# Hybrid decoder layer on one core: the output projection as seven products of quarters, and an order planned with GpSimd's and VectorE's shared port

## Chip, cores and metric

One core of a Trainium2 chip. The metric is the device time of one execution in microseconds (us). PE is TensorE's matmuls, PEld its weight loads, DVE is VectorE, ACT is ScalarE, POOL is GpSimd, SP is SyncE, which issues most of the DMAs.

## What is computed

One layer of a decoder for 1024 rows of 1024, in float32. Two attention mixers run beside each other; their outputs are projected, gated, merged, and projected again:

```python
h = rmsnorm(x, g_pre[i])
proj = h @ w_in[i]                              # queries, keys, values and gates of mixers A and B
y_a = (att_a * silu(gate_a)) @ w_branch_a[i]    # A: indexer, top-k keys, sparse attention
y_b = (att_b * silu(gate_b)) @ w_branch_b[i]    # B: forgetting attention
m_a, m_b = split(sigmoid(h @ w_merge[i]))
out = (m_a * y_a + m_b * y_b) @ w_out[i]        # the output projection, 1024x1024 @ 1024x1024
x = x + rmsnorm(out, g_post[i])
e = p[i] @ w_ple[i]
gate = sigmoid(x @ w_ple_gate[i])
x = x + rmsnorm(gate * e, g_ple[i])
```

## The kernel before

The kernel records every operation of the layer in a list (`Program`), plans an order for them, and only then issues them, all from one line (L521). So the profile's rows carry that line, and the tiles are parts of three arenas: `arena_r` (operands of matmuls), `arena_f` (float32) and `arena_p` (the eight PSUM banks).

Every matmul is done as three: a float32 operand is split into a rounded part `hi` (a cast, on ACT or DVE) and a rest `lo` (a subtraction, on POOL or DVE), and `mm3` adds `hi*hi + hi*lo + lo*hi` into one bank. Where two engines are given for an operation (`split_w`, `either`), the planner takes the one that finishes first by its costs (`_cost`). It keeps a free time per engine, and takes the earliest operation whose inputs, arena space and bank are there; the priority `BASE` of its part breaks ties. `QUOTA` bounds the space of each group of tiles: weights of the last stages (`wo`) have 56 KB, seven tiles, and their staging buffers (`st`) 8 KB, two of 4 KB.

The program goes: the projections and the indexer's scores (to about 260 us), four pairs of heads of mixer B with the top-k search beside them, mixer A with the merge gates `pm` filling PE between its steps, then the end, in which this order holds:

- branch projections, `y1_j_t` and `y0_j_t` for 8 column blocks j of the merged rows and 2 halves t of the rows: 4 x 3 matmuls each. DVE multiplies by the gates, adds, and the sum is split into `mt`. `at1...` are mixer B's results, loaded back by POOL's DMAs.
- the embedding `pe`, 16 blocks of 2 x 3 matmuls, stored in HBM (`ge_d`).
- the output projection `out{q}_{b}`: 2 halves q of the columns by 8 row blocks b, each 8 x 3 matmuls of 128x512. Its weights come in eight tiles, `wo0*` and `wo1*` (`load_q`), each half a float32 load of 512 KB, a cast and a subtraction. Per block DVE scales the bank into `x1` and ACT sums the squares. After q = 1 the block's residual follows: root, reciprocal, two scalings with the residual's addition in them, eight transposes `xt`, cast and difference into `xT`.
- the last gate `pg{q}_{b}`, again 2 x 8 blocks of 8 x 3 matmuls, with weights `wg0*` and `wg1*`, then the last norm and the stores.

The first gate blocks need `xT` of the first four row blocks alone. At the time of `pg0_0` the order before still has `xt7` ahead of it or in it.

## Time and profile before

| | |
|---|---|
| median of 3 runs | 1109.43 us (1109.23 to 1111.66) |
| profiled execution | 1111.12 us, its span 1109.4 us |
| PE / PEld busy | 97% / 80% of the span |
| DVE / ACT / POOL busy | 72% / 54% / 12% |
| DMA | 128.00 MB, 115 GB/s in the mean |
| mean granted clock of PE | 0.986 of full speed |

The span runs from the first to the last instruction. A busy share is a mean over stages with different limits. In the stage's tables each engine has its busy time and its number of instructions, PEclk is the granted clock (1.00 is 2.4 GHz, 0.50 is 1.2 GHz). In timelines a row merges operations of one kind that follow each other; in brackets stands the idle time of the engine ahead of them, and the engine whose work ended it. Operations of one engine overlap by some 0.08 us, so the distance between two starts tells what one costs in a queue.

### The profile page before, as it was taken

Reading aid. Unit: us, or ns where it says so; the run is one execution under the profiler, and the core shown is the slowest. Engines: PE = TensorE matmul, PEld = TensorE weight load, DVE = VectorE, ACT = ScalarE, POOL = GpSimd, SP = SyncE. Lnnn points to the kernel's source line nnn. Section 1 sums busy time; section 2 is a strip of 40 time slices with the busy share of each in tenths; the row PEclk is TensorE's granted clock in tenths of the full one; section 3 lists DMA queues with packets and bytes.
Section 4 is the critical chain, followed back from the end, with each engine's and each line's share of the span. In section 5 each row is a group of like instructions: output and inputs, shape, how many; then the busy total and the mean of one; then the engine's idle time right before and its main releaser. Section 6 shows DMA issues by size and latency. Waiting matters only on the chain. (4 is left out here: it accounts for less than half of the span.)

```text
span 1109.4 us, 16308 instructions
## 1 busy us (share of the span) xinstructions
PE 1073.3 (97%) x5290; PEld 882.7 (80%) x5290; DVE 802.1 (72%) x2086; ACT 603.8 (54%) x1396; POOL 133.2 (12%) x244
## 2 busy tenths in 40 slices
PE   8899999999999999999999999999999999999995
PEld 6777887887878878788878888888888888887884
DVE  6999667757969878799999957655388732366277
ACT  6565578888889889775278855432112131233212
POOL 1413000010111211211411200000100000000011
PEclk8999999999999999999999999999999999998998
DMA  7212033370361622635243422333786273026032
GB/s 264 70 37 67 11 138 119 134 180 10 102 156 39 159 70 82 150 97 178 95 124 97 122 64 79 106 113 106 227 247 200 77 242 109 29 72 202 31 111 99
DMA packets 117594, 128.00 MB, mean 115 GB/s; under 512 B 11642, under 2 KB 78330, under 8 KB 117508
## 3 DMA queue, kind: packets, MB, share of 16 engines
q1 hardware_dynamic: 105940, 108.60, 30.7%
q0 software_dynamic: 11568, 18.35, 7.1%
q8 instruction: 42, 0.69, 0.3%
q14 instruction: 44, 0.36, 0.1%
HBM read 89.60 MB, written 33.13 MB: 111 GB/s over the span
## 5 line engine op out<-in xcount | busy, mean ns | idle before, releaser
L521 PE MATMUL arena_p<-arena_r 128*128 128x512 f32 (+5 forms) x4384 | 1016.0, 385 | 17.1 <-DVE arena_r L521 6.5
L521 PEld LDWEIGHTS arena_p<-arena_r 128*128 128x128 f32 x4384 | 783.8, 190 | 175.6 <-DVE arena_r L521 11.3
L521 ACT ACTIVATE arena_f<-arena_p 128x512 f32<-128x512 f32 (+5 forms) x188 | 97.9, 533 | 205.9 <-PE arena_p L521 123.7
L521 DVE TENSOR_TENSOR arena_r<-arena_p,arena_r 128x512 fp32r<-128x512 f32 (+3 forms) x232 | 141.7, 622 | 48.4 <-ACT arena_r L521 44.7
L521 ACT CAST arena_r<-arena_p 128x512 fp32r<-128x512 f32 (+4 forms) x217 | 107.3, 516 | 117.7 <-PE arena_p L521 114.1
L521 ACT ACTIVATE arena_f<-arena_f,cnd 128x1024 bf16<-128x1024 f32 (+4 forms) x160 | 149.7, 936 | 31.9 <-DVE cnd L521 28.1
L521 ACT ACTIVATE arena_f<-arena_f,stats 128x512 f32<-128x512 f32 (+3 forms) x192 | 116.9, 611 | 21.2 <-DVE stats L521 15.8
L521 DVE TENSOR_TENSOR arena_r<-arena_f,arena_r 128x512 fp32r<-128x512 f32 (+4 forms) x200 | 120.0, 612 | 4.3 <-ACT arena_r L521 1.0
L521 PE MATMUL arena_p<-ident,arena_f 128*128 128x128 f32 x720 | 110.7, 276 | 1.8 <-DVE arena_r L521 0.6
L521 POOL TENSOR_TENSOR arena_r<-arena_f,arena_r 128x512 fp32r<-128x512 f32 (+2 forms) x51 | 65.4, 1289 | 366.2 <-ACT arena_r L521 111.4
L521 PEld LDWEIGHTS arena_p<-ident,arena_f 128*128 128x128 f32 x720 | 87.4, 142 | 24.0 <-DVE arena_f L521 2.3
L521 ACT CAST arena_r<-arena_f 128x512 fp32r<-128x512 f32 (+3 forms) x104 | 55.1, 561 | 69.2 <-DVE arena_f L521 45.8
L521 DVE CAST arena_r<-arena_f 128x512 fp32r<-128x512 f32 (+3 forms) x147 | 55.1, 384 | 41.5 <-DMA arena_f<-in_w_out_dram 15.2
L521 DVE CUSTOM_DVE_ANT_0 arena_f<-arena_p,arena_f 128x512 f32<-128x512 f32 (+2 forms) x112 | 64.1, 577 | 2.6 <-PE arena_p L521 1.5
L521 DVE SCALAR_TENSOR_TENSOR arena_f<-arena_f,wi 128x384 f32<-128x384 f32 (+3 forms) x70 | 48.3, 696 | 13.4 <-ACT arena_f L521 12.6
L521 POOL TENSOR_SCALAR_AFFINE_SELECT arena_f<-arena_f 128x128 f32<-128x128 f32 x70 | 22.5, 323 | 260.5 <-DVE stats L521 112.8
L521 DVE SCALAR_TENSOR_TENSOR arena_f<-arena_f,arena_p 128x512 f32<-128x512 f32 x48 | 32.8, 683 | 28.9 <-PE arena_p L521 22.1
L521 DVE CAST arena_r<-arena_p 128x512 fp32r<-128x512 f32 (+4 forms) x67 | 40.8, 612 | 17.7 <-PE arena_p L521 17.4
L521 ACT COPY arena_f<-arena_p 64x256 f32<-64x256 f32 (+5 forms) x85 | 37.8, 445 | 21.7 <-PE arena_p L521 17.9
L521 DVE SCALAR_TENSOR_TENSOR arena_f<-arena_f 128x512 f32<-128x512 f32 (+7 forms) x47 | 29.0, 623 | 26.5 <-ACT arena_f L521 25.6
L521 DVE TENSOR_TENSOR arena_f<-arena_f 128x512 f32<-128x512 f32 (+3 forms) x101 | 45.0, 446 | 1.3 <-DMA arena_f<-rd_d 0.5
L521 DVE CUSTOM_DVE_ANT_0 arena_f<-arena_p,arena_f,stats 128x384 f32<-128x384 f32 (+2 forms) x64 | 39.3, 615 | 6.9 <-PE arena_p L521 3.6
(103 smaller groups left out, 486.1 us busy)
## 6 DMA issues: line engine op xcount, KB each, us to landing
arena_f<-in_w_in_dram SPq DMA_DIRECT2D x56, 256.0 KB
arena_f<-in_w_merge_dram SPq DMA_DIRECT2D x32, 256.0 KB
th_d<-arena_f SPq DMA_DIRECT2D x32, 256.0 KB
arena_f<-th_d SPq DMA_DIRECT2D x32, 256.0 KB
arena_f<-in_x_dram SPq DMA_DIRECT2D x18, 256.0 KB
vb_d<-arena_r SPq DMA_DIRECT2D x8, 512.0 KB
qsa_d<-arena_r SPq DMA_DIRECT2D x16, 256.0 KB
arena_f<-negc_d SPq DMA_DIRECT2D x8, 512.0 KB
```

What stands on the lines that cost most here:

```text
L521: getattr(eng[x], m)(*[real(q) for q in a], **{n: real(q) for n, q in k.items()})
```

## The change

The output projection becomes seven products of quarters instead of eight. The merged rows are cut in four quarters of 512 x 512 (A11 is rows 0 to 511 by columns 0 to 511), the weights too (B11 ...). With the sums S1 = A21+A22, S2 = S1-A11, S3 = A11-A21, S4 = A12-S2 and T1 = B12-B11, T2 = B22-T1, T3 = B22-B12, T4 = B21-T2 the products P1 = A11 B11, P2 = A12 B21, P3 = S4 B22, P4 = A22 T4, P5 = S1 T1, P6 = S2 T2, P7 = S3 T3 are formed (four blocks of 128 rows each, 4 x 3 matmuls a block). The output's quarters are P1+P2, P1+P6+P5+P3, P1+P6+P7+P4 and P1+P6+P5+P7, added up on DVE, ACT and in PSUM: P2 is accumulated onto P1's banks after these were copied out, P4 onto P7's.

The sums of the rows are formed in the branch stage as its blocks come out. The sums of the weights are formed on POOL alone, 16 subtractions of 128x512 in four rounds through one tile of 8 KB, and stored in HBM (`tw_d`); each round's two loads of 512 KB also wait for a weight load of one of the last eight merge gates. The scaling by `g_post` moves from the PSUM read into the residual, whose addition becomes an operation of its own.

The planner gets a rule: an operation of DVE with SBUF inputs alone (with a few exceptions) and a two-input operation of POOL don't overlap in the plan. Some quotas grow (`wn`, `we`, `xr`), `vbt` gets its reserve earlier.

```diff
+def _port(eng, method, a, k):
+    ins = [q for q in list(a[1:]) + list(k.values()) if isinstance(q, Ref) and q is not k.get("out")]
+    big = [q for q in ins if q.shape[1:] != (1,)]
+    if eng == "G":
+        return method.startswith("tensor_") and len(big) > 1
+    if eng != "V" or any(q.t.space == "P" for q in ins) or method in ("memset", "tensor_tensor_reduce", "tensor_tensor_scan"):
+        return False
+    return len(big) > 1 or "accum_out" not in k
...
+        def starts(op, e):
+            s = max(free[e], op.r[e])
+            return max(s, port["G" if e == "V" else "V"]) if op.port[e] else s
...
-                    s = max(t0, op.r[e])
+                    s = starts(op, e)
...
+    def weight_sums(w, dst, after):
+        for k in range(4):
+            b4 = pg.tile([P, 4, 512], F32, "tw", f"tw{k}")
+            for g in range(2):
+                SY.dma_start(b4[:, 2 * g:2 * g + 2].rearrange("p a b -> p (a b)"), w[(4 * g + k) * P:(4 * g + k + 1) * P, :])
+                pg.ops[-1].deps.add(after[k])
+            G.tensor_sub(b4[:, 0], b4[:, 1], b4[:, 0])
+            G.tensor_sub(b4[:, 1], b4[:, 3], b4[:, 1])
+            G.tensor_sub(b4[:, 3], b4[:, 3], b4[:, 0])
+            G.tensor_sub(b4[:, 2], b4[:, 2], b4[:, 3])
+            SY.dma_start(dst[:, k], b4)
+    weight_sums(w_out[0], tw_d[0], gate_at[8:12])
...
-            V.tensor_add(ths[0], ths[0], ths[1])
-            split_w(ths[0], mt[t][0][j // 4][:, j % 4], mt[t][1][j // 4][:, j % 4])
+            m = mq[t][j]
+            V.tensor_add(m, ths[0], ths[1])
+            if t == 0:
+                left["A11" if j < 4 else "A12"].append(halves(m, "mA", f"mA{j}"))
+            elif j < 4:
+                either("tensor_sub", s3[j], mq[0][j], m)
+            else:
+                q = j - 4
+                either("tensor_add", mq[1][q], mq[1][q], m)
+                either("tensor_sub", mq[0][q], m, s3[q])
+                either("tensor_sub", mq[0][j], mq[0][j], mq[0][q])
...
+    for n, src in (("S2", mq[0][:4]), ("S1", mq[1][:4]), ("S4", mq[0][4:]), ("S3", s3), ("A22", mq[1][4:])):
+        for k in range(4):
+            left[n].append(halves(src[k], "mS", f"{n}{k}"))
...
+    ws, open_ = wquad("B11"), []
+    for i in range(4):
+        open_.append(product(left["A11"], i, ws, "P1", [x1[4 + i]]))
+        A.copy(part[i], open_[i])
+    ws = wquad("B21")
+    for i in range(4):
+        A.copy(x1[i][:, q0], product(left["A12"], i, ws, "P2", [x1[i]], open_[i]))
+        square(i, 0)
+    ws = wquad("T2")
+    for i in range(4):
+        add_to(part[i], product(left["S2"], i, ws, "P6"), part[i])
+    ws, ws2 = wquad("T1"), wquad("B22")
+    for i in range(4):
+        add_to(late[i], product(left["S1"], i, ws, "P5"), part[i])
+        add_to(x1[i][:, q1], product(left["S4"], i, ws2, "P3"), late[i])
+        square(i, 1)
+        first_residual(i)
+    ws, open_ = wquad("T3"), []
+    for i in range(4):
+        open_.append(product(left["S3"], i, ws, "P7"))
+        add_to(late[i], open_[i], late[i])
+        square(4 + i, 1)
+    ws = wquad("T4")
+    for i in range(4):
+        add_to(part[i], product(left["A22"], i, ws, "P4", (), open_[i]), part[i])
+        square(4 + i, 0)
+        first_residual(4 + i)
...
-        for k in range(KC):
-            mm3(ps, mt[t][0][k // 4][:, k % 4, bs], mt[t][1][k // 4][:, k % 4, bs], *wq[q][k],
-                k == 0, k == KC - 1, [x1[b]] if k == 0 else ())
-        V.scalar_tensor_tensor(x1[b][:, cq], ps, 0.25, gpb[:, cq], op0=ALU.mult, op1=ALU.mult)
-        A.activation(jo, ps, AF.Square, scale=0.25, accum_out=s1[:, b, q:q + 1])
```

`product` runs the 4 x 3 matmuls of one block, `add_to` adds a bank to a tile on DVE, `square` sums squares on ACT from `x1`, `first_residual` is the block's residual as above, `quad` loads and splits the two weight tiles of a quarter.

Where instructions stand now, at three places. First PE, from the last blocks of the output projection to the end. Rows of 128x128 are the transposes `xt` of the residual blocks, all others matmuls of the projection or, at the end, of the gate. Before:

```order
L521 MATMUL arena_p<-arena_r 128x512 x15
L521 MATMUL arena_p<-ident,arena_f 128x128 x4
L521 MATMUL arena_p<-arena_r 128x512 x9
L521 MATMUL arena_p<-ident,arena_f 128x128 x4
L521 MATMUL arena_p<-arena_r 128x512 x6
L521 MATMUL arena_p<-ident,arena_f 128x128 x4
L521 MATMUL arena_p<-arena_r 128x512 x21
L521 MATMUL arena_p<-ident,arena_f 128x128 x4
L521 MATMUL arena_p<-arena_r 128x512 x357
```

and now:

```order
L541 MATMUL arena_p<-arena_r 128x512 x12
L541 MATMUL arena_p<-ident,arena_f 128x128 x4
L541 MATMUL arena_p<-arena_r 128x512 x15
L541 MATMUL arena_p<-ident,arena_f 128x128 x4
L541 MATMUL arena_p<-arena_r 128x512 x15
L541 MATMUL arena_p<-ident,arena_f 128x128 x4
L541 MATMUL arena_p<-arena_r 128x512 x6
L541 MATMUL arena_p<-ident,arena_f 128x128 x4
L541 MATMUL arena_p<-arena_r 128x512 x324
```

384 matmuls belong to the gate. So the last transposes moved from 27 matmuls into the gate to 60 matmuls into it, two and a half blocks.

Second DVE at the hand-over. Rows of 128x1024 from `arena_f` are the splits of the gate's weights, rows of 128x512 from `arena_p` are reads of a product's bank, those of 128x4x128 differences for `xT`, `s_164` holds the sums of squares and what follows from them. Before:

```order
L521 SCALAR_TENSOR_TENSOR arena_f<-arena_p,arena_f 128x512
L521 TENSOR_TENSOR s_164<-s_164 128x1
L521 CAST arena_r<-arena_f 128x1024
L521 TENSOR_TENSOR arena_r<-arena_p,arena_r 128x4x128
L521 RECIPROCAL s_164<-s_164 128x1
L521 TENSOR_TENSOR arena_r<-arena_f,arena_r 128x1024
L521 SCALAR_TENSOR_TENSOR arena_f<-arena_f,s_164 128x512
L521 TENSOR_TENSOR arena_r<-arena_f,arena_r 128x1024
```

and now:

```order
L541 SCALAR_TENSOR_TENSOR arena_f<-arena_p,arena_f 128x512
L541 TENSOR_TENSOR arena_r<-arena_f,arena_r 128x1024 x2
L541 TENSOR_TENSOR arena_r<-arena_p,arena_r 128x4x128
L541 SCALAR_TENSOR_TENSOR arena_f<-arena_p,arena_f 128x512
L541 TENSOR_TENSOR arena_r<-arena_f,arena_r 128x1024
L541 SCALAR_TENSOR_TENSOR arena_f<-arena_p,arena_f 128x512
L541 TENSOR_TENSOR arena_r<-arena_f,arena_r 128x1024
```

The first bank read shown before is that of the last output block; the first one now is that of the third block of P7, with P4's four still to come. The weights' casts are on ACT now.

Third POOL, in the first part of the program, from the first two-input operation (a weight's or a query's rest) to mixer B's masks. Before:

```order
L521 TENSOR_TENSOR arena_r<-arena_f,arena_r 128x4x128
L521 TENSOR_TENSOR arena_r<-arena_f,arena_r 128x512 x9
L521 TENSOR_TENSOR arena_r<-arena_f,arena_r 128x4x64 x3
L521 AFFINE_SELECT arena_f<-arena_f 128x128
L521 TENSOR_TENSOR arena_r<-arena_f,arena_r 128x4x64
L521 AFFINE_SELECT arena_f<-arena_f 128x128
L521 TENSOR_TENSOR arena_r<-arena_f,arena_r 128x512
L521 TENSOR_TENSOR arena_r<-arena_f,arena_r 128x4x64
L521 TENSOR_TENSOR arena_r<-arena_f,arena_r 128x512
L521 AFFINE_SELECT arena_f<-arena_f 128x128
L521 TENSOR_TENSOR arena_r<-arena_f,arena_r 128x512 x3
L521 AFFINE_SELECT arena_f<-arena_f 128x128 x5
```

and now:

```order
L541 TENSOR_TENSOR arena_r<-arena_f,arena_r 128x4x128 x2
L541 TENSOR_TENSOR arena_r<-arena_f,arena_r 128x512 x3
L541 AFFINE_SELECT arena_f<-arena_f 128x128 x8
L541 DMA arena_r<-arena_r 64x2x512 x2
L541 DMA arena_r<-vb_d 128x4x256 x2
```

Of 20 such operations 5 are left; the others are DVE's. Later, 16 of `arena_f<-arena_f 128x512` join POOL's queue: four ahead of the next to last load of mixer B's first half, 12 ahead of the last.

## Rows read from the trace of the kernel before

**Rows 1.** Which engine is how busy: busy us, share of the span, instructions.

```profile
PE 1073.3 (97%) x5290; PEld 882.7 (80%) x5290; DVE 802.1 (72%) x2086; ACT 603.8 (54%) x1396; POOL 133.2 (12%) x244
```

**Rows 2.** Stages: PE, PEld, DVE, ACT, POOL busy (instructions), PEclk, DMA share, GB/s.

```profile
60.00:120.00 60.00, 57.67 (x287) 45.67 (x286) 53.17 (x147) 35.85 (x83) 13.30 (x14) 0.97 0.15 42
...
794.80:838.30 43.50, 43.50 (x193) 36.04 (x192) 33.18 (x55) 5.69 (x10) 2.59 (x2) 1.00 0.84 256
...
907.20:950.70 43.50, 43.50 (x193) 36.04 (x192) 10.41 (x13) 5.40 (x15) 0.00 (x0) 1.00 0.35 121
...
1096.30:1109.40 13.10, 0.00 (x0) 0.00 (x0) 7.28 (x19) 3.37 (x6) 1.48 (x2) 0.63 0.23 82
```

**Rows 3.** PE's timeline at its gaps: start, us, operation, idle before and releaser.

```profile
42.81 0.73 PE L521 MATMUL arena_p<-identr,arena_r 128*128 128x128 f32 x4 [2.69 <-DVE arena_r L521]
...
109.40 0.62 PE L521 MATMUL arena_p<-arena_r 128*128 128x384 f32 x2 [1.89 <-ACT arena_f L521]
...
262.61 7.58 PE L521 MATMUL arena_p<-arena_r 128*128 128x384 f32 x28 [2.41 <-DVE arena_f L521]
...
1004.56 0.80 PE L521 MATMUL arena_p<-arena_r 128*128 128x512 f32 x1 [2.34 <-DVE arena_r L521]
1005.75 2.50 PE L521 MATMUL arena_p<-arena_r 128*128 128x512 f32 x5 [0.40 <-DVE arena_r L521]
```

**Rows 4.** Stages of the lower clock, columns as in rows 2.

```profile
263.50:266.90 3.40, 3.40 (x11) 2.95 (x10) 1.55 (x7) 3.37 (x10) 0.39 (x2) 0.50 0.00 0
...
1004.20:1011.00 6.80, 6.05 (x15) 4.51 (x16) 4.53 (x7) 1.06 (x2) 0.00 (x0) 0.50 0.84 286
```

**Rows 5.** DVE's timeline at the hand-over to the last gate.

```profile
1001.60 0.69 DVE L521 SCALAR_TENSOR_TENSOR arena_f<-arena_p,arena_f 128x512 f32<-128x512 f32 x1
...
1003.21 0.69 DVE L521 CAST arena_r<-arena_f 128x1024 fp32r<-128x1024 f32 x1
...
1004.49 1.21 DVE L521 TENSOR_TENSOR arena_r<-arena_f,arena_r 128x1024 fp32r<-128x1024 f32 x1
```

**Rows 6.** POOL's timeline, five places.

```profile
34.52 6.08 POOL L521 TENSOR_TENSOR arena_r<-arena_f,arena_r 128x512 fp32r<-128x512 f32 x4
...
103.93 3.25 POOL L521 TENSOR_TENSOR arena_r<-arena_f,arena_r 128x512 fp32r<-128x512 f32 x2 [3.08 <-DVE arena_r L521]
...
403.32 2.52 POOL L521 TENSOR_TENSOR arena_r<-arena_f,arena_r 128x512 fp32r<-128x512 f32 x2 [20.18 <-DVE cur L521]
...
701.69 0.56 POOL L521 DMA_DIRECT2D arena_r<-att_d  x1
...
857.40 1.30 POOL L521 TENSOR_TENSOR arena_r<-arena_f,arena_r 128x512 fp32r<-128x512 f32 x1 [28.57 <-DVE arena_r L521]
```

**Rows 7.** DVE's timeline beside the first three of these.

```profile
39.38 1.40 DVE L521 TENSOR_TENSOR arena_f<-arena_f,cs 128x8 f32<-128x8 f32 x3
...
104.38 1.66 DVE L521 SCALAR_TENSOR_TENSOR arena_f<-arena_f,wi 128x384 f32<-128x384 f32 x1
...
403.70 0.68 DVE L521 SCALAR_TENSOR_TENSOR arena_f<-arena_f,arena_p 128x512 f32<-128x512 f32 x1
```

**Rows 8.** DVE's timeline, operations that follow each other, and a scaling.

```profile
855.47 0.69 DVE L521 TENSOR_TENSOR arena_r<-arena_f,arena_r 128x512 fp32r<-128x512 f32 x1
856.07 0.68 DVE L521 TENSOR_TENSOR arena_f<-arena_f 128x512 f32<-128x512 f32 x1
...
960.38 1.41 DVE L521 SCALAR_TENSOR_TENSOR arena_f<-arena_f,s 128x512 f32<-128x512 f32 x2
```

**Rows 9.** Pieces of the chain that ended last: start, us, what.

```profile
887.64 4.70 DMA arena_f<-in_w_out_dram
...
1004.57 1.13 DVE arena_r L521
```

**Rows 10.** PE's timeline, small waits in the last stages.

```profile
899.17 61.93 PE L521 MATMUL arena_p<-arena_r 128*128 128x512 f32 x272 [0.23 <-DVE arena_r L521]
...
976.93 0.66 PE L521 MATMUL arena_p<-ident,arena_f 128*128 128x128 f32 x4 [0.26 <-DVE arena_r L521]
```

More of the change, by code (lines that the diff above doesn't have):

```diff
@@ L464, in schedule @@
             free[e] = s + c
+            if op.port[e]:
+                port[e] = s + c
             if hasattr(op, "dma"):
@@ L1252, in hybrid_block_kernel, with halves @@
     mixer_a()
-    mt = [[[pg.tile([P, 4, 512], F32R, f"m{t}", f"m{t}{e}{g}") for g in range(2)] for e in range(2)] for t in range(2)]
+    def halves(src, grp, name):
+        hl_ = [pg.tile([P, 512], F32R, grp, f"{name}{e}") for e in range(2)]
+        split_w(src, *hl_)
+        return hl_
+    mq = [[pg.tile([P, 512], F32, "mq", f"mq{t}{j}") for j in range(8)] for t in range(2)]
+    s3 = [pg.tile([P, 512], F32, "mq", f"ms{j}") for j in range(4)]
+    left = {n: [] for n in ("A11", "A12", "S1", "S2", "S3", "S4", "A22")}
     for t in range(2):
@@ new lines, in product, with square @@
+    def product(lw, i, ws, name, hold=(), onto=None):
+        ps = onto or pg.psum([P, 512], "d", f"{name}_{i}")
+        begun.append(len(pg.ops))
+        for k in range(4):
+            h_, l_ = lw[k]
+            bs = slice(i * P, (i + 1) * P)
+            mm3(ps, h_[:, bs], l_[:, bs], *ws[k], k == 0 and not onto, k == 3, hold if k == 0 else (), again=onto is not None)
+        return ps
+    def square(b, q):
+        A.activation(jo, x1[b][:, q * 512:q * 512 + 512], AF.Square, scale=0.25, accum_out=s1[:, b, q:q + 1])
@@ new lines, in add_to, with wquad @@
+    def add_to(out_, ps, part):
+        V.scalar_tensor_tensor(out_, ps, 1.0, part, op0=ALU.mult, op1=ALU.add)
+    def wquad(n):
+        return quad(w_out[0], tw_d[0], n)
+    q0, q1 = slice(0, 512), slice(512, 1024)
+    part, late = [x1[4 + i][:, q0] for i in range(4)], [x1[4 + i][:, q1] for i in range(4)]
+    ws, open_ = wquad("B11"), []
[3 more added lines that the diff above has]
+    ws = wquad("B21")
```

83 lines of the change are left out of this document (50 added, 33 removed), and 6 rows, old and new, of the table QUOTA.

## Prediction

> **What bounds the kernel now.** I read the page's totals first, then a table of stages, then the engines' rows around every place where TensorE stood still. TensorE (PE) is busy for 1073.3 of 1109.4 us [rows 1]: everything else matters only where PE waits for it. The table of stages shows how little there is of that: in 794.80 to 838.30, and again in 907.20 to 950.70, inside the output projection, PE is busy for the whole 43.50 us, with 192 weight loads each, so one 128x512 matmul costs 43.50/192 = 226.6 ns at the full clock [rows 2]. The 36.1 us in which PE isn't busy are the 13.1 us behind its last matmul [rows 2], 1.1 us ahead of its first, and about 22 us of gaps. The largest that I can name are four: 2.69 us at 40 us and 1.89 us at 107.5 us, 2.41 us at 260.2 us, and 2.34 + 0.40 us at 1002 to 1005.8 us, at the hand-over from the output projection to the last gate [rows 3]. After three of these the granted clock falls to 0.50, its lower level of 1.2 GHz: for 6.8 us at 1004.2, for 3.4 us at 263.5, and a third time, like the second, for 3.4 us at 109.9 [rows 4]. Half a clock loses half of that time: 3.4, 1.7 and 1.7 us.
>
> **The change, part by part.** The sum is made against the profiled execution: 1111.1 us with its span of 1109.4. The median of the runs is 1109.4 us, 1.7 us lower, and I take the same difference off from that.
>
> *Matmuls.* The output projection had 16 blocks of 8 x 3 = 24 matmuls, 384. Seven quarter products have 4 blocks of 4 x 3 = 12 each: 336. That is 48 x 226.6 ns = 10.9 us off a stage in which PE waits for nothing [rows 2]. This has one answer. The Trainium skill (TensorE: Matmul & The Clock Gate, Back-to-back issue gap) gives about 131 ns as the sustained pitch of 512-column matmuls; by that the saving would be 6.3 us. The trace says 226.6 ns, and that decides.
>
> *The hand-over to the last gate.* Before, the 2.74 us gap is a wait for the split of the gate's first weights: the cast at 1003.21 and the subtraction at 1004.49 stand on DVE behind the PSUM read of the last output block at 1001.60 and the block's small sums [rows 3, 5]. In the new order the four subtractions of those weights stand ahead of most PSUM reads of the last product, that is some 10 us ahead of the gate, and the transposes of the last residual blocks stand behind one to two gate blocks, which don't need them. So this gap and its slow clock, 2.7 + 3.4 = 6.1 us, should go. Bounds: 0 to 6.1 us gained; I take 6.1, since nothing that the gate's first block needs is issued late any more. What is late next is the transposes of row blocks 4 to 7, which wait for DVE (below).
>
> *GpSimd off the shared port.* The rows show what a collision costs: while GpSimd (POOL) subtracts two SBUF tensors from 34.52 to 40.60, DVE's multiplications of 8 columns take 1.40 us for three, and PE's transposes behind them come 2.69 us late; while it does so from 103.93 to 107.18, an operation of 384 columns takes 1.66 us, more than twice what DVE needs for 512, and PE waits 1.89 us [rows 3, 6, 7]. A DVE operation that reads PSUM takes its usual 0.68 us beside POOL, at 403.70 [rows 6, 7]. In the new order POOL has 5 subtractions instead of 20 before the pairs start, and those around both gaps are on DVE, behind the operations that PE waits for. At most 2.69 + 1.89 + 1.7 = 6.3 us come back, at least nothing: 16 subtractions move (one goes the other way), 11 of 512 columns at 0.60 us apart [rows 8] and 5 of half the size, about 8 us more on a DVE that is busy for 53.17 of 60 us in 60 to 120 us [rows 2], even though the collisions are part of that. I take 3.0 us. The gap at 260 us I leave: DVE's order around it is the same, word for word.
>
> *Splits, quarter sums and weight sums.* Twelve more splits of quarters, 16 sums and differences of the merged rows, six more weight tiles. In the branch stage DVE is busy for 33.18 of 43.50 us [rows 2]; a pair of products there gets at most three quarter sums of 0.60 us and loses its subtraction of the split, against 24 x 226.6 ns = 5.4 us of PE. Free, as long as DVE stays below PE's pace. The weight tiles come through two staging buffers: 4.70 us to land, cast and subtraction at 0.69 + 1.13 us [rows 5, 9], about 6.5 us each, 3.3 us per tile with two buffers, against 24 matmuls = 5.4 us per tile. Also covered. I put 6 changes of quarter at the wait of 0.23 us with which the embedding's second half begins [rows 10], 1.4 us; bounds 0 to 3.
>
> *Weight sums on POOL.* Sixteen sums at 1.30 us [rows 6], 20.8 us, in four rounds: load, four sums, store, through one buffer. They stand ahead of the load of the last piece of mixer B's first half, which POOL issued at 701.69 before [rows 6] and which the first branch block reads, at 794.8 [rows 2]. If the two loads land one after the other and the store takes as long, a round is 9.4 + 5.2 + 9.4 = 24 us; if they overlap, 4.7 + 5.2 + 4.7 = 14.6. Four rounds are 58 to 96 us, and the first load stands where that issue at 701.69 stood: 93 us of room. I cost it at nothing. By the Trainium skill (GPSIMD Engine Reference, Engine selection) elementwise additions of two tensors belong on VectorE, since GpSimd is about half as fast; on DVE the 16 would be 16 x 0.60 = 9.7 us of a queue that has room there, so the sum is the same either way.
>
> *The residual on a fuller DVE.* This is the new cost. Per row block PE has 24 matmuls and 8 transposes, 5.4 + 0.8 = 6.2 us. DVE has two PSUM additions, two scalings at 0.70 us [rows 8], two residual additions (one per half was part of the scaling before), two differences for the transposes, small ones: 5.2 us, and with the weight splits and the last halves, 13.8 us over eight blocks, 6.9 us. So DVE falls behind by about 0.7 us a block, 5 to 6 us at the end of the last product; the order allows for that, with block 7's transposes two gate blocks later than the last product. PE then meets up to 16 transposes that wait for DVE. Before, such waits were at most 0.26 us [rows 10]. I take 16 x 0.2 = 3.2 us; bounds 0, and 8 us if PE takes over DVE's whole lag and some of the chain through ScalarE.
>
> *The end.* DVE's last 110 operations, and the 13.1 us behind PE's last matmul, stay.
>
> Sum: -10.9 - 6.1 - 3.0 + 1.4 + 3.2 = -15.4 us. The profiled execution would be 1095.7 us, the median **1094.0 us**.
>
> **Rivals.**
>
> *Only the matmuls.* The waits that go are replaced by others of their size: the list of operations is planned anew over the whole program, and one late split before a product gives 2.7 us and 3.4 us of slow clock as at 1004 us. For it: DVE has next to no slack in the last stage. Against: the pairs' order is mostly unchanged, and products have an early weight load. Time: 1109.4 - 10.9 + 0 to 6 = 1098.5 to 1105 us.
>
> *DVE sets the pace from the fifth product on.* If DVE's operations follow each other at their full durations, 0.69 and 1.21 us [rows 5, 8], and not at their pitch of 0.60 and 1.13, as they do where each waits for another engine, a block is 6.9 x 0.69/0.60 = 7.9 us against PE's 6.2: 1.7 us of wait per block, 14 us over eight, in gaps like those after which the clock fell; with half the clock for a fifth of the 65 us another 6 us. Gains at the hand-over go too, as DVE gets there late. 1109.4 - 10.9 - 3 + 1.4 + 14 + 6 = 1117 us, slower than before. The point is DVE's work per block above PE's 6.2 us without room to catch up behind it; here it is 6.9 with two gate blocks, 11 us, behind. The Trainium skill speaks for this one: matmul groups that cycle through PSUM banks leave short idle times between groups, between which the clock goes down and up (TensorE: Matmul & The Clock Gate, A second HAM failure mode: psum-queue depth-cycling). The groups here halve from 24 to 12 matmuls. Before, with 24, no row in the projection shows it: the clock is 1.00 [rows 2].
>
> *The weight sums come late.* At 24 us a round, POOL issues the last piece of B's result at about 800 us, it lands 4.7 us later, and the first branch block waits some 8 us, with 3.4 us of slow clock: 1094 + 11 = 1105 us. It decides at rounds of 22 us.
>
> *The gaps close further.* All 6.3 us of collisions gone and no waits at the transposes: 1109.4 - 10.9 - 6.1 - 6.3 = 1086 us.
>
> **How the numbers follow.** Forecast (1089 to 1098) 0.58; only the matmuls 0.19; gaps close further (1084 to 1089) 0.11; weight sums late 0.04; DVE's pace 0.08. A measurement of this kernel tells about 0.2%, 2.2 us, from no change. Faster: the first three and most of the fourth, 0.90; same 0.02; slower 0.08. The range of 8 in 10 leaves out the slow rival, the late sums and the lowest edge: 1086 to 1105 us.
>
> **What would show it.** Right: 48 fewer 128x512 matmuls (336 between the embedding and the gate), still about 227 ns apart; PE without a gap of over 1 us at 40, 107 and at the hand-over, and no half clock in the last 200 us but at the very end; gap at 260 us as before; POOL with some 20 us of sums between 700 and 775 us, PE not idle at its first branch block; small waits at the transposes of the residual blocks, under 4 us together. Wrong: DVE busy for over 95% of the seven products with PE gaps after each; PE waiting for DMA of the summed weights at the second or third quarter; a clock of 0.50 anywhere in the products; or new waits of microseconds in the first 120 us, where DVE takes over POOL's subtractions.

## The result, and the profile after

The changed kernel takes **1085.02 us** (median of 4 runs, 1084.51 to 1085.32), the one before 1109.6 us (4 runs): a ratio of 0.9774, 95% interval 0.9757 to 0.9791, some 24.6 us. The forecast was 1094.0 us with a range from 1086 to 1105, so the time lies 1 us below it. The direction and most places were right, the size was not: against the 1109.4 us that the forecast started from, 24.4 us were gained where 15.4 were worked out.

The totals of the page of the changed kernel, to be held against [rows 1]:

```profile
PE 1054.9 (97%) x5242; PEld 869.2 (80%) x5242; DVE 826.6 (76%) x2139; ACT 633.1 (58%) x1447; POOL 129.0 (12%) x239
```

48 instructions fewer on PE, as worked out, and 18.4 us less of its busy time. The stages (columns as in [rows 2]: the branch projections, the products up to the first residual, the rest of the products, the last gate, what follows PE's last matmul):

```profile
756.70:877.70 121.00, 120.95 (x540) 100.08 (x538) 80.74 (x140) 20.41 (x38) 4.80 (x9) 1.00 0.63 191
...
900.70:946.20 45.50, 45.50 (x202) 37.64 (x201) 27.24 (x35) 14.66 (x27) 1.29 (x1) 1.00 0.54 180
946.20:981.40 35.20, 35.20 (x176) 29.44 (x175) 32.34 (x56) 20.25 (x44) 1.29 (x1) 1.00 0.41 133
981.40:1071.50 90.10, 90.09 (x409) 74.22 (x407) 59.18 (x146) 26.75 (x51) 5.54 (x6) 1.00 0.30 101
1071.50:1083.10 11.60, 0.00 (x0) 0.00 (x0) 5.77 (x13) 3.38 (x6) 2.02 (x2) 0.71 0.32 111
```

In the branch stage and the products PE is busy for all but 0.05 us, at the full clock, and a matmul still costs 45.50/201 = 226 ns. PE's timeline at the places of [rows 3]: the transposes at 40 us, the scores at 107.5 us, the gap at 260 us, and a new one:

```profile
38.65 0.47 PE L541 MATMUL arena_p<-identr,arena_r 128*128 128x128 f32 x4
```

```profile
98.16 10.01 PE L541 MATMUL arena_p<-arena_r 128*128 128x384 f32 x42
```

```profile
250.11 2.14 PE L541 MATMUL arena_p<-arena_r 128*128 128x384 f32 x5 [2.39 <-DVE arena_f L541]
```

```profile
722.79 1.42 PE L541 MATMUL arena_p<-arena_r 128*128 128x512 f32 x5 [1.70 <-DVE arena_r L541]
```

No idle time is left in brackets at the first two, the gap of 2.4 us stands as it did, and one of 1.70 us at 721 us is new. The hand-over to the last gate, at 981.4 us, has no gap at all, and the clock is 1.00 on both sides of it.

The table adds up PE's idle time from all its records, by stage (up to mixer B's first pair, mixers B and A, branch stage to the last gate), for the two kernels and for six others that the next section explains. All columns but the first are of the one profiled execution, whose own time stands second; it is not always near the median. "Half clock" is half of PE's busy time in stretches with a granted clock of 0.50. "Stretched" is what DVE's operations took above the median of the operations with the same name, tiles and shape in the same trace, and in brackets the part of it in operations that overlap a two-input operation of POOL. POOL is the number of its operations with two SBUF inputs.

| kernel | us, median | us, profiled | up to the pairs | B and A | branch to gate | half clock | behind PE | stretched | POOL |
|---|---|---|---|---|---|---|---|---|---|
| before | 1109.4 | 1111.1 | 9.9 | 9.2 | 3.9 | 9.6 | 13.1 | 23.5 (20.7) | 59 |
| after | 1085.0 | 1084.8 | 4.1 | 12.4 | 0.1 | 3.4 | 11.6 | 13.1 (9.9) | 54 |
| rule only (e2) | 1110.4 | 1108.6 | 5.9 | 14.9 | 4.1 | 3.4 | 11.6 | 11.7 (8.7) | 37 |
| products only (e1) | 1115.1 | 1116.8 | 10.2 | 13.4 | 13.9 | 11.9 | 10.7 | 39.4 (36.1) | 86 |
| products only, second plan (e9) | 1103.5 | 1099.4 | 8.4 | 16.2 | 5.1 | 3.4 | 10.7 | 38.5 (35.1) | 87 |
| products only, third plan (e9) | 1100.3 | 1100.6 | 9.5 | 10.1 | 4.0 | 6.8 | 13.2 | 37.7 (34.7) | 87 |
| both, second plan (e8) | 1088.2 | 1088.1 | 4.3 | 13.9 | 1.1 | 1.7 | 11.6 | 11.2 (7.3) | 56 |
| both, third plan (e8) | 1083.8 | 1083.5 | 3.9 | 13.3 | 0.0 | 3.4 | 11.6 | 7.7 (4.0) | 57 |

Before against after: 10.9 us of matmuls, 5.8 + 3.8 us of gaps, 6.2 of half clock and 1.5 behind PE are gained, and 3.2 lost in the stages of mixers B and A: 25.0 of the 26.3 us between the two spans. The other 1.3 us I can't place.

### The profile page after: what moved, and what is told of

It is laid out like the page before. It is cut to its first block, busy times and chain, and to the rows that moved or that the text cites. A ratio compares the mean times of both kernels' runs of the same rounds, so it can differ in the third digit from the quotient of the medians.

```text
span 1083.1 us, 16343 instructions
## 1 busy us (share of the span) xinstructions
PE 1054.9 (97%) x5242; PEld 869.2 (80%) x5242; DVE 826.6 (76%) x2139; ACT 633.1 (58%) x1447; POOL 129.0 (12%) x239
## 3 DMA queue, kind: packets, MB, share of 16 engines
q1 hardware_dynamic: 109300, 120.13, 34.7%
## 5 line engine op out<-in xcount | busy, mean ns | idle before, releaser
L541 PE MATMUL arena_p<-arena_r 128*128 128x512 f32 (+4 forms) x4336 | 999.1, 384 | 12.8 <-DVE arena_r L541 5.4
L541 DVE TENSOR_TENSOR arena_r<-arena_p,arena_r 128x512 fp32r<-128x512 f32 (+2 forms) x232 | 142.5, 623 | 44.6 <-ACT arena_r L541 41.0
L541 ACT CAST arena_r<-arena_p 128x512 fp32r<-128x512 f32 (+3 forms) x217 | 107.4, 513 | 105.2 <-PE arena_p L541 97.0
L541 ACT ACTIVATE arena_f<-arena_f,cnd 128x1024 bf16<-128x1024 f32 (+4 forms) x160 | 149.6, 935 | 23.5 <-DVE cnd L541 19.2
L541 ACT ACTIVATE arena_f<-arena_p 128x512 f32<-128x512 f32 (+4 forms) x172 | 88.8, 527 | 125.5 <-PE arena_p L541 118.8
L541 DVE TENSOR_TENSOR arena_r<-arena_f,arena_r 128x512 fp32r<-128x512 f32 (+5 forms) x240 | 146.0, 623 | 11.2 <-PE arena_p L541 4.6
L541 ACT CAST arena_r<-arena_f 128x512 fp32r<-128x512 f32 (+3 forms) x144 | 80.7, 584 | 90.3 <-DVE arena_f L541 35.2
L541 PEld LDWEIGHTS arena_p<-ident,arena_f 128*128 128x128 f32 x720 | 86.4, 140 | 23.5 <-DVE arena_f L541 2.7
L541 POOL TENSOR_TENSOR arena_r<-arena_f,arena_r 128x512 fp32r<-128x512 f32 (+1 forms) x29 | 39.2, 1355 | 336.0 <-ACT arena_r L541 261.3
L541 DVE CAST arena_r<-arena_f 128x512 fp32r<-128x512 f32 (+4 forms) x125 | 47.8, 390 | 31.6 <-DMA arena_f<-in_w_out_dram 9.7
L541 DVE TENSOR_TENSOR arena_f<-arena_f 128x512 f32<-128x512 f32 (+3 forms) x132 | 64.9, 496 | 4.1 <-DMA arena_f<-rd_d 3.0
L541 POOL TENSOR_TENSOR arena_f<-arena_f 128x512 f32<-128x512 f32 (+1 forms) x25 | 29.9, 1197 | 189.3 <-ACT arena_f L541 103.1
L541 DVE SCALAR_TENSOR_TENSOR arena_f<-arena_f,arena_p 128x512 f32<-128x512 f32 x48 | 32.9, 685 | 23.5 <-PE arena_p L541 18.5
```

What stands on the lines that cost most here:

```text
L541: getattr(eng[x], m)(*[real(q) for q in a], **{n: real(q) for n, q in k.items()})
```

## Experiments

My theory after the result: the products give 17 us (matmuls and hand-over), the rule the two early gaps with their clock, 6.3 us, and both simply add. The rival: every new plan of the whole list moves gaps about, and the excess over the forecast is luck.

**The two halves apart.** Products without the rule (e1):

```diff
         def starts(op, e):
             s = max(free[e], op.r[e])
-            return max(s, port["G" if e == "V" else "V"]) if op.port[e] else s
+            return s
```

> The seven products with everything that belongs to them, planned without the rule on the shared port. Theory: the rule is worth the two early gaps (2.69 + 1.89 us) and the half clock behind the second (1.7 us), and nothing else; without it POOL takes its early subtractions back and both gaps return: 1085.0 + 6.3 = 1091.3 us, while the hand-over to the last gate stays closed, since its weights' splits still stand early on DVE. Rival: the excess over the forecast comes from the new plan of the whole list, not from the port; then gaps of the same total stand at other places, and the time is within 2 us of 1085.

Measured: 1115.07 us against 1110.19 on the same chip, 1.0031 (1.0016 to 1.0046): *slower than before* (by 4.9 us in the medians), and 24 us over what the theory expected, further still from the rival's 1085. Both early gaps came back (2.75 and 1.75 us), but they are the small part. PE's timeline in the branch stage:

```profile
825.86 3.04 PE L541 MATMUL arena_p<-arena_r 128*128 128x512 f32 x12 [0.90 <-DVE arena_r L541]
829.95 2.56 PE L541 MATMUL arena_p<-arena_r 128*128 128x512 f32 x10 [1.05 <-DVE arena_r L541]
833.63 0.73 PE L541 MATMUL arena_p<-arena_r 128*128 128x512 f32 x2 [1.12 <-DVE arena_r L541]
834.83 18.05 PE L541 MATMUL arena_p<-arena_r 128*128 128x512 f32 x70 [0.47 <-DVE arena_r L541]
853.75 0.70 PE L541 MATMUL arena_p<-arena_r 128*128 128x512 f32 x2 [0.87 <-DVE arena_f L541]
856.17 4.14 PE L541 MATMUL arena_p<-arena_r 128*128 128x512 f32 x10 [1.72 <-DVE arena_r L541]
```

What POOL and DVE did just ahead of the first of these:

```profile
820.81 1.33 POOL L541 TENSOR_TENSOR arena_f<-arena_f 128x512 f32<-128x512 f32 x1 [13.98 <-DMA arena_f<-in_w_out_dram]
822.41 4.55 POOL L541 TENSOR_TENSOR arena_f<-arena_f 128x512 f32<-128x512 f32 x3 [0.28 <-POOL arena_f L541]
```

```profile
821.03 1.66 DVE L541 TENSOR_TENSOR arena_r<-arena_f,arena_r 128x512 fp32r<-128x512 f32 x1
822.61 0.67 DVE L541 SCALAR_TENSOR_TENSOR arena_f<-arena_f,arena_p 128x512 f32<-128x512 f32 x1
...
824.16 1.65 DVE L541 TENSOR_TENSOR arena_r<-arena_f,arena_r 128x512 fp32r<-128x512 f32 x1
825.73 0.68 DVE L541 SCALAR_TENSOR_TENSOR arena_f<-arena_f,arena_p 128x512 f32<-128x512 f32 x1
826.44 1.07 DVE L541 TENSOR_TENSOR arena_f<-arena_f 128x512 f32<-128x512 f32 x1
```

POOL works on the last round of the weight sums with hardly a pause. In this plan the sums run from 768 to 827 us and so into the branch stage; in the five other plans of the products, with the rule or without it, the last one ends by 767 us. DVE's subtraction of 128x512 takes 1.66 and 1.65 us instead of 0.69, its addition 1.07; the operations that read PSUM, in the rows between, 0.67 and 0.68 as always. The subtraction at 824.16 is the split that PE waits for at 825.86. So the collisions of [rows 6, 7] come in the new work too, where I had looked for none. The last two gaps, 0.87 and 1.72 us, have no POOL operation beside them, since POOL issues none from 827 to 877 us, and DVE's operations there take their usual 0.69 us: that part belongs to the order of this plan.

The old kernel with the rule alone (e2): `_port`, `starts` and their three uses, as in the change, nothing else.

> The kernel before with the rule on the shared port alone; the output projection is the old one, and on DVE the split of the last gate's first weights stands behind the last output block as before. Theory: the gaps at 40 and 107 us go with their half clock, the gap and the 6.8 us of half clock at the hand-over stay: 1109.5 - 6.3 = 1103.2 us. Rival (the products closed these gaps, or a new plan moves gaps about): within 2 us of 1109.5.

Measured: 1110.39 against 1110.19 us, 1.0002 (0.9989 to 1.0015): no change, as the rival said. PE at the three places that matter:

```profile
37.24 0.59 PE L541 MATMUL arena_p<-identr,arena_r 128*128 128x128 f32 x4
```

```profile
439.31 1.97 PE L541 MATMUL arena_p<-arena_r 128*128 128x512 f32 x5 [2.26 <-DVE arena_r L541]
```

```profile
1004.45 0.49 PE L541 MATMUL arena_p<-arena_r 128*128 128x512 f32 x1 [2.52 <-DVE arena_r L541]
```

The early gap went and the hand-over's stayed, both as expected, yet the time did not follow: 4.0 us less in the early stages and 1.5 behind PE stand against 5.7 us more in the stages of mixers B and A, of which 439.31 is the largest piece. The profiled execution, 2.5 us below that of the kernel before and among the fastest of ten (1108.2 to 1113.4 us), also has 6.2 us less of half clock; 3.3 us the other way I can't place. So in these plans the parts do not add: alone they cost 0.2 and 4.9 us, together they gain 24.6. The rule alone was tried in this one plan, so how much of its nothing is bad luck stays open.

**Luck or rule.** One plan of each kind can't tell a rule from luck. So I had the planner make two more of each, with one number changed that has nothing to do with the port (by how many ns ScalarE may prefer a more urgent operation):

```diff
-SLACK = {"T": 0, "V": 0, "A": 80, "G": 0, "S": 0}
+SLACK = {"T": 0, "V": 0, "A": 60, "G": 0, "S": 0}
```

and 100 in the other pair, with the rule (e8) and without it (e9).

> The changed kernel planned anew with one number that has nothing to do with the change set otherwise (by how many ns ScalarE may prefer a more urgent operation: 60 instead of 80), rule on. PE's order differs from its 412th operation on. Theory (the rule itself keeps the time down, whatever the order): 1081 to 1092 us, gaps of PE in the branch, embedding and output stages together under 3 us. Rival (the 30 us between the kernels with and without the rule are the luck of one plan): anywhere between 1085 and 1115 us, as the plans without the rule.

> As the last, with 100 ns: PE's order differs from its 238th operation on. Theory: 1081 to 1092 us, gaps in the last stages under 3 us. Rival: anywhere between 1085 and 1115 us.

> The seven products without the rule, the same number at 60 instead of 80. Theory (without the rule POOL takes 86 two-input operations instead of 54, and they stretch DVE's where PE waits for it): 1103 to 1120 us, with over 8 us of gaps in the branch, embedding and output stages, and both early gaps at 40 and 106 us. Rival (luck): as likely below 1095 us as above.

> As the last, with 100 ns. Theory: 1103 to 1120 us, with over 8 us of gaps in the branch, embedding and output stages. Rival: as likely below 1095 us as above.

Measured: with the rule 1088.16 and 1083.81 us, without it 1103.47 and 1100.32, against 1109.67 before on the same chip (0.9808, 0.9769, 0.9953, 0.9918, each within 0.003). Six plans do not overlap: 1083.8 to 1088.2 with the rule, 1100.3 to 1115.1 without. By the medians luck is worth some 4 us among plans with the rule and 15 without, where two of the plans also spread by 6 to 7 us from run to run; e1 was an unlucky plan; my bound of 8 us for the gaps of the last stages was too high for the other two, that of 1103 us for the one with 100. The rule, beside the products, is worth 12 to 31 us, 21 in the mean (15 to 30 between two plans with the same number). The table shows where: early stages 4 us against 8 to 10, branch to gate 0 to 1 against 4 to 14, DVE stretched by 8 to 13 us against 38 to 39.

The rule does two things: it lays the operations of the two engines apart, and it leaves fewer on POOL, 54 to 57 instead of 86 or 87. Fewer is not all of it: per operation of POOL the stretch beside it is 0.40 to 0.42 us without the rule and 0.07 to 0.18 with it. How much of the time each of the two is worth, no run separates.

What a typical wait of the plans without the rule is made of, in the third, at the embedding: POOL, DVE and PE.

```profile
892.21 2.21 POOL L541 TENSOR_TENSOR arena_r<-arena_f,arena_r 128x512 fp32r<-128x512 f32 x1 [0.58 <-DVE arena_r L541]
894.78 3.89 POOL L541 TENSOR_TENSOR arena_r<-arena_f,arena_r 128x512 fp32r<-128x512 f32 x2 [0.36 <-DVE arena_r L541]
```

```profile
893.18 1.52 DVE L541 CAST arena_r<-arena_f 128x512 fp32r<-128x512 f32 x1
894.62 2.92 DVE L541 TENSOR_TENSOR arena_r<-arena_f,arena_r 128x1024 fp32r<-128x1024 f32 x2
897.46 0.68 DVE L541 COPY arena_f<-arena_p 128x512 f32<-128x512 f32 x1
```

```profile
898.19 2.11 PE L541 MATMUL arena_p<-arena_r 128*128 128x512 f32 x8 [1.45 <-DVE arena_f L541]
```

POOL splits the quarter sums S2 and S1. DVE's cast beside it takes 1.52 us instead of 0.41, the two subtractions behind it (the second of 128x512) 2.92 instead of 1.21 + 0.69. The bank that PE needs is read at 897.46, and PE has stood for 1.45 us. In all three plans without the rule PE waits there for 1.45 us, in none with it.

**Is it the collision, or the new plan?** The plan of before stays, instruction for instruction, but six of POOL's subtractions go to DVE, behind what PE waits for (e3; the numbers are places in the recorded list, the first four the rests of the query weights, the last two those of the value weights):

```diff
+def _edit(pg, moves, engines):
+    for n, e in engines:
+        pg.ops[n].eng = e
+    for n, after in moves:
+        pg.order.remove(pg.ops[n])
+        pg.order.insert(pg.order.index(pg.ops[after]) + 1, pg.ops[n])
...
     pg.schedule()
+    _edit(pg, [(414, 231), (417, 232), (420, 263), (423, 295), (887, 635), (890, 656)], [(414, 'V'), (417, 'V'), (420, 'V'), (423, 'V'), (887, 'V'), (890, 'V')])
```

> The plan of the kernel before, instruction for instruction, but with six subtractions (four of the second query weights at 34 to 41 us, two of mixer B's value weights at 104 to 107 us) taken from POOL to DVE, each put behind the small operations that PE waits for. Nothing is planned anew. Theory (the collision on the port makes both gaps): DVE's operations of 8 columns take 0.16 us again instead of 1.25, the gap at 40 us shrinks from 2.69 to under 0.5 us, the one at 107 from 1.89 to under 0.7 us, and its half clock goes: 1109.5 - 5 = 1104.5 us. Rival (DVE's queue is late by its own work, and POOL is no matter): gaps of 2 us each stay, within 1.5 us of 1109.5.

Measured: 1106.05 against 1110.19 us, 0.9961 (0.9946 to 0.9975): 4.1 us, one less than expected. DVE at the row that answers to [rows 7], and PE behind it:

```profile
36.56 0.32 DVE L529 TENSOR_TENSOR arena_f<-arena_f,cs 128x8 f32<-128x8 f32 x3
```

```profile
40.42 0.47 PE L529 MATMUL arena_p<-identr,arena_r 128*128 128x128 f32 x4
...
50.56 0.28 PE L529 MATMUL arena_p<-identr,arena_r 128*128 128x128 f32 x1 [1.08 <-DVE arena_r L529]
```

```profile
106.98 0.62 PE L529 MATMUL arena_p<-arena_r 128*128 128x384 f32 x2 [0.38 <-ACT arena_f L529]
...
110.92 0.54 PE L529 MATMUL arena_p<-identr,arena_r 128*128 128x128 f32 x4 [1.56 <-ACT arena_f L529]
```

Three multiplications of 8 columns take 0.32 us instead of 1.40, and the gap of 2.69 us is gone. At 107 us 0.38 is left of 1.89. Two other gaps took their place, 1.08 and 1.56 us, each where a further POOL subtraction now meets DVE (POOL's run from 48.69 for 1.33 us and from 107.49 for 1.79). So the collision makes those gaps, and taking some POOL operations away by hand moves most of the cost to the next ones: in the profiled execution, the slowest of the four, PE's idle time up to the pairs falls only from 9.9 to 9.4 us. The 3.1 us between the two spans are mostly clock: 1.7 us are the half clock behind the second gap, which is gone, and another 1.5 a shorter one at the hand-over, which the edit doesn't touch. In this stage the rule does better than six moves (5.9 us idle in e2), in the whole time it did not (1110.4 us).

**The hand-over put back (e4).** The changed plan, with two DVE copies of a weight rest onto itself ahead of the last gate's first block (`lo` is the rest of `wg00`):

```diff
+    lo = pg.ops[5210].var[-1][1][0][1][0]
+    calls = next(c for e, c in pg.ops[5156].var if e == "V")
+    calls += [("tensor_copy", (lo, lo.bitcast(F32)), {})] * 2
```

> The changed kernel's plan, with two more DVE copies of a weight rest onto itself (128x1024, about 0.7 to 1.2 us each) just ahead of the last gate's first block, so that this block's first weights are ready late, as in the kernel before. Theory (the hand-over was worth its gap and the half clock behind it): PE stands for 2 to 3 us at the first gate block and the clock falls to 0.50 for 3.4 to 6.8 us: 1085.0 + 4 to 6.5 = 1089 to 1091.5 us. Rival (such a wait is made up later, since DVE and not PE holds the gate): under 1.5 us more.

Measured: 1086.28 us, 0.9782 (0.9760 to 0.9803), not to be told from the changed kernel by its time. The copies, the gap and the stretch around it:

```profile
980.48 1.41 DVE L547 CAST arena_r<-arena_r 128x1024 fp32r<-128x1024 f32 x2
```

```profile
981.95 0.73 PE L547 MATMUL arena_p<-arena_r 128*128 128x512 f32 x2 [1.20 <-DVE arena_r L547]
```

```profile
981.00:985.00 4.00, 3.05 (x15) 2.52 (x16) 3.96 (x9) 0.78 (x2) 0.00 (x0) 1.00 0.68 229
985.00:992.00 7.00, 7.00 (x36) 5.83 (x35) 6.51 (x13) 5.72 (x9) 0.00 (x0) 1.00 0.34 113
```

The copies took 1.41 us in all, less than I had given them, so this wait was 1.20 us and not 2 to 3. In this execution the granted clock stays at 1.00 behind it, so the dose was too small to try the theory, and the time, 1.3 us more, proves neither side. Two of the four runs, 1087.33 and 1089.3 us, have a mean clock of 0.991 instead of 0.995; where they lost it no profile shows. Behind the wait of 2.34 + 0.40 us in [rows 3] it fell, and so it did in e2 and e3, where the stretch at 0.50 was 3.4 us and not the 6.8 of [rows 4].

**How much slack does DVE have in the products (e5)?** All 16 differences for `xT` done twice:

```diff
+    for op in pg.order:
+        for e, calls in op.var:
+            if e == op.eng == "V" and calls[0][0] == "tensor_sub" and isinstance(calls[0][1][0], Ref):
+                if calls[0][1][0].t.name[:4] in ("xT01", "xT11"):
+                    calls.append(calls[0])
```

> The changed kernel's plan with every one of the 16 PSUM subtractions for the gate's transposed operand done twice on DVE: 16 x 0.60 = 9.6 us more of DVE, nearly all between 946 and 1000 us, where DVE was busy for 47.3 of 51.6 us. Theory (in the changed kernel PE never waited for DVE there because the transposes stand behind other matmuls by more than DVE's lag; that slack is under 2 us for most of them): PE now waits at the transposes, 4 to 10 us with the half clock behind the gaps: 1089 to 1095 us. Rival (the cover is deep, two gate blocks of 11 us): under 1.5 us more.

Measured: 1093.0 us, 0.9850 (0.9834 to 0.9865), 8 us more than the changed kernel. PE at two of the transposes, and the stretches around them (in the changed kernel the 51.60 us from 946.20 have DVE busy for 47.34 and PE for all):

```profile
993.83 0.66 PE L552 MATMUL arena_p<-ident,arena_f 128*128 128x128 f32 x4 [1.12 <-DVE arena_f L552]
...
1002.60 0.66 PE L552 MATMUL arena_p<-ident,arena_f 128*128 128x128 f32 x4 [0.79 <-DVE arena_f L552]
```

```profile
962.00:984.00 22.00, 20.39 (x98) 15.53 (x97) 21.79 (x39) 11.77 (x25) 1.31 (x1) 1.00 0.31 100
984.00:1004.00 20.00, 17.80 (x86) 13.84 (x85) 19.76 (x34) 12.13 (x20) 0.00 (x0) 1.00 0.53 169
```

DVE is busy without a pause, and PE waits for it. From the first product to the last matmul this kernel takes 6.5 us longer than the changed one, 4.0 us of them in gaps of PE, the rest in longer rows. (Up to the first product the two profiled executions differ by 0.5 us, although this one has 3.4 us of the lower clock behind the gap at 721 us, which was 2.64 us this time.) So 9.6 us more on DVE cost 6.5 us: there is some 3 us of slack. The plans without the rule have 9 to 12 us of stretched DVE operations from the embedding to 16 us into the gate, where the changed kernel has 1.1, and take 2.4 to 4.2 us longer than it from the first product to the last matmul: a like dose, a smaller effect.

**The weight sums on DVE (e6).** The 16 operations change their engine, at their places in the order:

```diff
+    for op in pg.order:
+        if op.eng == "G" and op.var[0][1][0][0] == "tensor_sub" and op.var[0][1][0][1][0].t.name[:2] == "tw":
+            op.var = [("V", op.var[0][1])]
+            op.eng = "V"
```

> The changed kernel's plan with the 16 weight sums on DVE instead of POOL, each in the same place of the order. Theory: the gap of 1.70 us at 721 us is a collision of POOL's second round of sums with two DVE operations (1.31 and 1.35 us instead of 0.28) ahead of a split that PE waits for; on DVE the four sums cost 4 x 0.60 = 2.4 us at the same place, which is as late, and DVE also waits for the loads: the gap stays between 1 and 3 us, within 2 us of 1085. Rival (DVE has room, and the sums belong there): the gap goes, 1083 us.

Measured: 1084.35 us, 0.9769 (0.9754 to 0.9784). The rival was right about the gap; the time fits both. Ahead of the gap at 722.79, POOL and DVE in the changed kernel, then DVE in this one:

```profile
701.27 5.40 POOL L541 TENSOR_TENSOR arena_f<-arena_f 128x512 f32<-128x512 f32 x4 [21.26 <-DMA arena_f<-in_w_out_dram]
...
717.47 5.79 POOL L541 TENSOR_TENSOR arena_f<-arena_f 128x512 f32<-128x512 f32 x4 [7.41 <-DMA arena_f<-in_w_out_dram]
...
746.86 5.40 POOL L541 TENSOR_TENSOR arena_f<-arena_f 128x512 f32<-128x512 f32 x4 [9.33 <-DMA arena_f<-in_w_out_dram]
```

```profile
719.21 1.45 DVE L541 CAST arena_r<-arena_f 128x128 fp32r<-128x128 f32 x2
720.58 1.56 DVE L541 TENSOR_TENSOR arena_r<-arena_f,arena_r 128x128 fp32r<-128x128 f32 x2
722.06 0.68 DVE L541 TENSOR_TENSOR arena_r<-arena_p,arena_r 128x512 fp32r<-128x512 f32 x1
```

```profile
719.09 0.36 DVE L551 CAST arena_r<-arena_f 128x128 fp32r<-128x128 f32 x2
719.36 0.49 DVE L551 TENSOR_TENSOR arena_r<-arena_f,arena_r 128x128 fp32r<-128x128 f32 x2
719.76 0.69 DVE L551 TENSOR_TENSOR arena_f<-arena_f 128x512 f32<-128x512 f32 x1
720.37 0.69 DVE L551 TENSOR_TENSOR arena_r<-arena_p,arena_r 128x512 fp32r<-128x512 f32 x1
```

The casts take 0.36 instead of 1.45 us, the subtractions 0.49 instead of 1.56, and the split that PE waits for starts 1.28 us behind the first cast instead of 2.85, although one of the sums (719.76, 0.69 us) now stands between them. The gap is gone; a gap of 0.58 us is new at 709 us. In time it is 0.7 us, within the noise. The rule should have laid these operations apart; on the chip they met. POOL's round began when its loads landed (7.41 us idle, ended by the DMA), so they probably landed at another time than in the plan, whose times no run shows.

**By hand (e7, e10).** In the changed plan the bank that PE waits for at 250.11 is freed by a tanh on ACT and a product on DVE which stand behind the top-k search's operations. e7 puts them ahead, and the split of 721 us ahead of the operations that collide:

```diff
+    for n, after in ((1876, 1875), (1877, 1876), (2291, 1877), (2296, 2291), (4282, 4087), (4283, 4282)):
+        pg.order.remove(pg.ops[n])
+        pg.order.insert(pg.order.index(pg.ops[after]) + 1, pg.ops[n])
```

> The changed kernel's plan with two places changed by hand: at 246 us the tanh and the product that read a bank PE waits for stand ahead of the top-k search's operations on ACT and DVE instead of behind them, and at 719 us a split that reads PSUM stands ahead of the four DVE operations that collide with POOL's weight sums. Theory: the gap of 2.39 us at 247.7 us falls under 0.5 and its half clock (1.7 us) goes, the gap of 1.70 us at 721 us goes: 1085.0 - 2.1 - 1.7 - 1.7 = 1079.5 us. Rival (the search's chain comes late in their place, or the waits come back at the next block): within 1.5 us of 1085.

Measured: 1082.9 us (1079.54 to 1083.87 in five runs), 0.9750 (0.9734 to 0.9765). PE at the place, and the start of the program with that place:

```profile
248.49 1.68 PE L547 MATMUL arena_p<-arena_r 128*128 128x384 f32 x7 [0.90 <-DVE stats L547]
250.83 2.37 PE L547 MATMUL arena_p<-arena_r 128*128 128x384 f32 x10 [0.67 <-DVE stats L547]
```

```profile
7.00:17.80 10.80, 8.57 (x69) 7.44 (x68) 8.28 (x14) 9.49 (x20) 2.52 (x2) 1.00 1.02 335
247.00:254.00 7.00, 5.44 (x25) 3.90 (x24) 6.22 (x22) 6.93 (x19) 1.16 (x4) 1.00 0.00 0
```

The wait of 2.39 us became two of 0.90 and 0.67, and behind neither of them the granted clock fell (1.00 in the second row, 0.76 in the changed kernel). That the clock was saved by the shorter waits isn't shown: in e6 the 2.39 us stand as they did, and the clock behind them is 1.00 too. The gap at 721 us is 0.31. The expected 1079.5 us are reached in two of the five runs, the profiled one among them, with a mean clock of 0.996 and 0.997; the other three have 0.993. One place where runs differ is the start: here the clock is 1.00 from 7 to 17.8 us, in the changed kernel's profile 0.84, in e10's 0.68, with the same order of PE's instructions there. This alone moves a run by up to 3 us.

e10 combines the sums on DVE, the first of the two moves and a third like it at 301 us.

> The changed kernel's plan with three places changed by hand, as far as the runs before point to them: the 16 weight sums on DVE, at 246 us the tanh and the product for the bank that PE waits for ahead of the top-k search, at 301 us the same for a query block's two tanh. Theory: the gap at 721 us goes (1.7), the one at 247.7 shrinks to 0.9 and its half clock goes in most executions (1.5 + 0 to 1.7), the one at 305 us goes (0.7): 1085.0 - 3.9 to 5.6 = 1079.4 to 1081.1 us. Rival (these waits come back at the next block, as at 250 us where the first of them was moved before): 1083 to 1085 us.

Its start:

```profile
7.00:17.80 10.80, 7.61 (x37) 6.91 (x38) 6.01 (x10) 6.56 (x13) 2.50 (x2) 0.68 0.96 306
```

Measured: 1083.42 us, 0.9761 (0.9747 to 0.9775): the rival. The moved waits came back in part at the next blocks (0.79 + 0.99 us at 306 to 311 us where one of 0.68 had been). By their medians such moves gain 1.6 to 2.1 us, which is not clear of the noise: e7 is the fastest version of all, and its interval still overlaps that of the changed kernel.

## Why the prediction was wrong in size, point by point

Two places of the sum were mis-sized. The port was put at -3.0 us, and the two gaps and their clock gave 6.3. The new waits, at quarter changes (+1.4) and transposes (+3.2), came to less than 0.1 us. That is 7.9 of the 9.0 us by which the sum was beaten; the rest are small pieces in both directions. The first term gave half of the gain away to the subtractions that move to DVE, and DVE had the room. The second took DVE's lag to reach PE: DVE is busy for 47.34 of the 51.60 us from 946.20, with some 3 us to spare (e5), and PE waits nowhere. Without the rule, with the same products, it does, and this the sum could not see, since it costed the rule by the stalls of the old trace alone.

- **Matmuls, -10.9: right.** 48 instructions fewer, 226 ns each. The rival taken from the Trainium skill (TensorE: Matmul & The Clock Gate, A second HAM failure mode: psum-queue depth-cycling) did not come: with groups of 12 matmuls the granted clock in the products is 1.00.
- **Hand-over, -6.1: right** for these two profiles (2.74 us of gaps and 6.8 us of half clock, both 0 now). The half clock behind the same wait was 3.4 us in e2 and e3, so the place is worth 4.4 to 6.1 us. It belongs to the products: e2 keeps the gap, and e1, without the rule, has none at its first gate block.
- **The port, -3.0: the step that failed, twice over.** First its value: I took the middle between 0 and 6.3 since the subtractions add 8 us to DVE. Both gaps went wholly, with their clock, -6.3; DVE did not suffer: from 60 to 120 us it is busy for 51.78 us, against 53.17 before, with the subtractions moved to it, since operations that are no longer stretched leave the room (e3: 0.32 us instead of 1.40). Second its scope: I costed the rule against the collisions that the old trace showed. The products bring DVE and POOL new operations with SBUF inputs, and without the rule these collide as well: 38 to 39 us of stretched DVE time against 23.5 before. Beside the products the rule is worth 12 to 31 us.
- **Quarter changes, +1.4, and transposes, +3.2: 0.** PE idles for less than 0.1 us from the branch stage to its last matmul. The 4.6 us were not far off for a kernel *without* the rule: there the same stages, from the first product to the last matmul, take 2.4 to 4.2 us longer than in the changed kernel, 1.4 to 3.1 of it in gaps. With the rule the transposes stand behind enough matmuls. That is a narrow thing: e5 shows that 9.6 us more on DVE bring 4.0 us of gaps.
- **Splits and quarter sums, "free, as long as DVE stays below PE's pace": right by the result, wrong as a reason.** In e1 DVE was busy for 13.14 of the 16 us from 820 to 836, so it had time to spare, and PE still waited 3.5 us there. A share doesn't tell what one late split costs.
- **Weight sums on POOL, 0: nearly.** The four rounds start 14.7 to 16.2 us apart, the low end of my 14.6 to 24, and end at 752 us. But one round meets DVE ahead of a split, 1.70 us at 721 us. The Trainium skill (GPSIMD Engine Reference, Engine selection) would have them on VectorE; e6 agrees as to the gap, and its time can't tell.
- **What I left out.** At the start the clock was 0.50 for 6.8 us before, which is not among [rows 4], and for 3.4 after: 1.7 us, which also differ between kernels that start alike. The end behind PE is 11.6 us instead of 13.1; it is 10.7 to 13.4 from plan to plan. The stages of mixers B and A lost 3.2 us, 1.7 of it at 721 us. None of these was in the sum, and they cancel (1.7 + 1.5 - 3.2 us): that is luck.
- **The rivals.** "Only the matmuls", 1098.5 to 1105 us, is what the products without the rule give in two of three plans. "The gaps close further", 1086 us, is what came, by its own mechanism (all 6.3 us of collisions, no waits at the transposes), and had 0.11.

What I should have read differently stood in the change itself: a rule for two engines, and new work for just these two. I summed them as if each stood alone.

## What to carry over

Cost a scheduling rule against the work that the new program has, not against the stalls of the old trace: where one part of a change loads the resource that another part guards, the parts need not add (0.2 us lost by the rule alone, in one plan; 4.9 lost to 9.4 gained by the products alone; 24.6 gained together). Where a planner lays a whole program anew, look at two or three plans of each kind before a difference of 5 us is put down to the change; here luck was worth 4 us among three plans with the rule and 15 among three without it. And where PE is full, look for the one late operation ahead of it, not at the busy share of the engine that issues it.

## What I had not expected of the hardware

A collision can cost DVE most of a POOL operation (1.0 to 1.1 us, where POOL's subtraction takes 1.30), whatever its own size: 0.16 us became 1.25, 0.69 became 1.66, a one-input cast 0.41 became 1.52, while PSUM reads of 128x512 in the same stretch took 0.67 and 0.68 us. The Trainium skill says so (SBUF — State Buffer, SBUF: two separate sides: the port pair that the two engines share is locked for a whole instruction, and the other engine waits); the traces agree, for operations with two inputs in SBUF and for casts. POOL pays as well: that subtraction of 128x512, 1.30 us alone, takes 2.21 us at 892.21 in the third plan without the rule. So a POOL operation that is "free" off the critical path can hold one on it up for 1 us, and behind some of PE's waits that follow from it stood 3.4 us at the lower clock (at 109.9 us in the kernel before, at 835.7 us in e1).
